# Quarter ends of an MLP: the next pair's first product moved between two parts of the last pair, and weight preparation moved behind the last minimum

## The chip, the cores and the metric

The kernel runs on one core of one Trainium2 chip. The metric is the time of one execution on the device, in microseconds (us); less is better. Engines are named as in the profile: PE is the matrix engine (matmuls; PEld its weight loads), DVE the vector engine, ACT the scalar engine, POOL and SP the two engines that mostly issue transfers here.

## The reference

One step of a two-layer encoder with model width 1024 and 576 tokens (512 of a prompt, 64 of a running stream). Layer 0 mixes tokens by causal pooling, layer 1 by sparse attention; each is followed by an MLP, and the change is in the MLP alone:

```python
def _mlp(h, w_up, w_down):          # w_up (1024, 4096), w_down (4096, 1024)
    u = jax.nn.relu(h @ w_up)
    return (u * u) @ w_down
...
x = x + _mlp(_rmsnorm(x, norm_mlp[i]), mlp_w_up[i], mlp_w_down[i])
```

## The kernel before

**Precision.** Every fp32 matmul is made of three: weights and operands are split into a high part (a cast) and a low part (value minus high part), and PE computes wh·uh, wh·ul and wl·uh. The cast is ACT's (for weights line 181, for activations `upper`, line 470), the subtraction DVE's (line 182 and `lower`, line 473). A weight *unit* is one 128x512 tile `wh` with its `wl`. There are six buffers for units (`UNITS = 6`), so the cast of a unit into `wh` waits until PE has read the unit six places earlier for the last time. `ahead()` makes the next unit if fewer than five (`LEAD`) stand ready, `take()` hands the oldest to a product.

**Seven products.** A 2x2 block product (halves of 576 tokens by pairs of weight blocks) is made by seven products instead of eight, named by the factor of the operand: b11, t1, t2, b21, t3, b22, t4. `seven()` issues them for one pair into three PSUM banks a, b and c: b11 into b (copied to a, line 530), t1 into c, t2 into b, then b21 into a, t3 into b, b22 into c, t4 into b. Each product is 4 k-parts (`rows`) of 3 matmuls of 128x288. A sink `on` takes the banks out when they are whole: `on.c`, `on.b`, `on.lo0`, `on.hi1`, `on.hi0`, `on.lo1`.

**Quarters.** The hidden width is worked in quarters c = 0 to 3. In c = 1 to 3 four `Up` pairs make activations (bank, times the norm, relu by a max or a min, square on ACT) and the operand `u` with its seven factors. `u` of pair j serves k-part j of the products of the `Down` pairs that follow, four of them (three for the last quarter of the last layer), which add to and subtract from the residual x (`update`, line 559). The end of a quarter is where the last `Up` pair (`final`) hands over to the first `Down` pair: that pair's products need `u` of the `Up` pair that is just being finished, so its k-part 3 comes late (`late`). There, t1 and t2 have their k-parts 0 to 2 first. There are six such ends: c = 1, 2, 3 in each of two layers. In the profiled execution they lie at 186, 277, 369, 834, 926 and 1017 us.

**Order.** Each engine works its own instructions in the order in which the program has them, and waits at one until its semaphores are there. The order is fixed when the program is built: a scheduler takes the operations by the order in which the code makes them and by what they depend on. The code's `with tc.issue_after(x)` puts what is made in it behind x on x's engine. Rows of the order below carry buffer numbers: at the end of the second quarter, `b_3498` (before) or `b_3504` (after) is the last `Up` pair's bank b, `b_3653`, `a_3654`, `c_3655` are the banks of the first `Down` pair, `u_3497` or `u_3503` is the operand that the last `Up` pair makes and `v_3496` or `v_3502` its values.

Of the kernel before, what the change touches and what calls it, by code (L numbers as in the profile page):

```python
# [12 lines left out]
ALU = mybir.AluOpType  # L13
# [43 lines left out]
def pool_dsa_kernel(ctx: ExitStack, tc: tile.TileContext, a, o):  # L57
# [53 lines left out]
    def f32(t):  # L111
        return t.bitcast(F32)
# [284 lines left out]
    def mlp(layer, gi, late=0, end=None):  # L397
# [74 lines left out]
        def lower(u, v, f):  # L472
            dve.tensor_tensor(u[:, f, 1], v[:, f], f32(u[:, f, 0]), ALU.subtract)  # L473

        def parts_of(u, v, f):

            upper(u, v, f)
            lower(u, v, f)

# [16 lines left out]
        def product(bank, w, operand, factor, js, first=False):  # L496
            for j in js:
                wh, wl = (t[:, j * P:(j + 1) * P] for t in w)
                uh, ul = (operand(j, factor, part) for part in range(2))
                for i, (wt, ut) in enumerate(((wh, uh), (wh, ul), (wl, uh))):  # L500
                    pe.matmul(bank[:, :HT], wt, ut, start=first and j == 0 and i == 0, stop=j == 3 and i == 2,  # L501
                              skip_group_check=True)

        tasks = [0]

        def ahead(n=1):

            how["sub"] = dve
            for _ in range(n):
                if len(ready) < LEAD:  # L510
                    u = next(units, None)
                    if u is not None:
                        ready.append(u)
# [6 lines left out]
        def seven(operand, late, on):  # L520
# [4 lines left out]
            w = take()  # L525
            product(b, w, operand, "b11", rows, True)
            tasks[0] += 1
# [5 lines left out]
            if late:  # L533
# [4 lines left out]
                on.c()  # L538
                ahead()
                product(b, w2, operand, "t2", rows[3:])  # L540
# [7 lines left out]
            for bank, factor, then in ((a_, "b21", on.lo0), (b, "t3", on.hi1), (c, "b22", on.hi0), (b, "t4", on.lo1)):  # L548
                product(bank, take(), operand, factor, rows)
                then()  # L550

        class Down:


            def __init__(self, q):
                self.lo, self.hi = ([x[2 * q + i][:, c0:c0 + HT] for i in range(2)] for c0 in (HT, 0))

            def update(self, to, bank, op):
                dve.tensor_tensor(to, to, self.banks[bank], op)  # L559

# [22 lines left out]
        class Up:  # L583
# [6 lines left out]
            def relu(self, i, src, op, h):  # L590
                v = self.v[:, i]
                dve.scalar_tensor_tensor(v, src, 0.0, halves(norm.rb)[:, h], op, ALU.mult)
                square(v)

            def c(self):
# [5 lines left out]
            def lo0(self):  # L601
                self.relu(4, self.banks[0], ALU.max, 1)
                ahead()
                if self.final:
                    parts_of(self.u, self.v, slice(4, 5))

            def hi1(self):
                v = self.v
                dve.tensor_tensor(v[:, 5], self.banks[1], snap[:, 0], ALU.add)  # L609
                self.relu(5, v[:, 5], ALU.min, 0)  # L610
                ahead()
# [11 lines left out]
            def lo1(self):  # L623
                v = self.v
                self.relu(6, self.banks[1], ALU.min, 1)
                if not self.final:
                    ahead()
                parts_of(self.u, v, slice(1, 4))
                last_sum(v)
                if not self.final:  # L630
                    ahead()
                parts_of(self.u, v, slice(0, 7, 6))
                if self.final:
                    ahead(2)

# [67 lines left out]
        for c in range(1, 4):  # L703
# [5 lines left out]
            if c < 3:  # L709
                for q in range(half):  # L710
                    seven(of(us), q == 0, Down(q))
        for q in range(pairs(3)):
            seven(of(us), q == 0, Down(q))
        if end:
# [865 lines left out]
```

## Time and profile before

| what | value |
|---|---|
| time, median of 3 runs | 1085.38 us (1085.03 to 1087.36) |
| profiled execution | 1086.18 us, with a span of 1084.4 us |
| PE busy | 1052.2 us, 97% of the span |
| DVE busy | 905.4 us, 83% |
| ACT busy | 627.7 us, 58% |
| mean granted clock of PE | 0.994 |

Times in rows are counted from the start of the span. The profiled execution took 1.8 us more than its span. PE is busy for all but 32 us, so only time in which PE waits, or in which its clock is lower, can be won; whether another engine is long busy matters only where PE waits for it. Matmuls overlap in the records: one takes 0.29 us, but the next starts 0.13 us after it.

### The profile page before, as it was taken

Reading aid. Unit: us, or ns where it says so; the run is one execution under the profiler, and the core shown is the slowest. Engines: PE = TensorE matmul, PEld = TensorE weight load, DVE = VectorE, ACT = ScalarE, POOL = GpSimd, SP = SyncE. Lnnn points to the kernel's source line nnn. Section 1 sums busy time; section 2 is a strip of 40 time slices with the busy share of each in tenths; the row PEclk is TensorE's granted clock in tenths of the full one; section 3 lists DMA queues with packets and bytes.
Section 4 is the critical chain, followed back from the end, with each engine's and each line's share of the span. In section 5 each row is a group of like instructions: output and inputs, shape, how many; then the busy total and the mean of one; then the engine's idle time right before and its main releaser. Section 6 shows DMA issues by size and latency. Waiting matters only on the chain.

```text
span 1084.4 us, 21653 instructions
## 1 busy us (share of the span) xinstructions
PE 1052.2 (97%) x7942; PEld 1024.4 (94%) x7942; DVE 905.4 (83%) x1837; ACT 627.7 (58%) x1240; POOL 263.9 (24%) x285
## 2 busy tenths in 40 slices
PE   9999999999999999999989999999999999999996
PEld 8999999999999999999979888999999999999895
DVE  7889889879978987869998944689889879979974
ACT  8556457447546654444477776456467447547641
POOL 3200111111111100227687892000111111111001
PEclk9999999999999999999999999999999999999998
DMA  8233776676676654456642454443775776676512
GB/s 252 91 100 89 173 163 160 162 164 165 154 165 166 156 161 165 126 155 186 200 113 66 136 161 127 126 108 89 175 162 150 172 167 164 152 170 157 128 50 88
DMA packets 94460, 157.66 MB, mean 145 GB/s; under 512 B 13730, under 2 KB 25297, under 8 KB 94353
## 3 DMA queue, kind: packets, MB, share of 16 engines
q1 hardware_dynamic: 68720, 109.80, 33.1%
q0 software_dynamic: 15840, 28.84, 17.4%
q10 hardware_dynamic: 9792, 17.63, 5.3%
q8 instruction: 62, 1.02, 0.4%
q14 instruction: 46, 0.37, 0.1%
HBM read 141.15 MB, written 10.89 MB: 140 GB/s over the span
## 4 chain that ended last, share of the span: by engine, by line
PE 78%; DVE 8%; DMA 4%; ACT 3%; issue 3%; POOL 2%; SPq 1%; DVEq 0%; POOLq 0%; ACTq 0%
PE b L501 29%; PE c L501 15%; PE up L305 9%; PE a L501 7%; PE pj L305 5%; PE wo L305 2%; PE wa L305 2%; DVE wl L182 2%; PE pb L1005 1%; PE pt L1304 1%; PE sc L1278 1%; PE o L1336 1%; PE dn L305 1%; DMA raw<-in_w_in 1%; DMA raw<-in_w_down 1%
## 5 line engine op out<-in xcount | busy, mean ns | idle before, releaser
L181 ACT CAST wh<-raw 128x512 fp32r<-128x512 f32 (+1 forms) x316 | 194.8, 620 | 250.8 <-PE b L501 84.4
L182 DVE TENSOR_TENSOR wl<-raw,wh 128x512 fp32r<-128x512 f32 (+1 forms) x294 | 206.1, 703 | 38.6 <-ACT wh L181 29.2
L501 PE MATMUL b<-u,wh 128*128 128x288 f32 x992 | 202.2, 296 | 3.6 <-ACT a L530 3.2
L501 PEld LDWEIGHTS b<-u,wh 128*128 128x128 f32 x992 | 159.0, 188 | 6.0 <-ACT a L530 6.0
L181 ACT CAST wh<-sum 128x512 fp32r<-128x512 f32 x165 | 101.7, 620 | 81.3 <-PE b L501 42.3
L501 PE MATMUL b<-u,wl 128*128 128x288 f32 x496 | 145.3, 295 | 0.0
L182 DVE TENSOR_TENSOR wl<-sum,wh 128x512 fp32r<-128x512 f32 x165 | 111.9, 687 | 26.3 <-ACT wh L181 24.0
L238 POOL DMA_DIRECT2D sum<-in_w_down x31 | 27.1, 891 | 329.0 <-DVE u L473 119.3
L501 PE MATMUL c<-u,wh 128*128 128x288 f32 x496 | 102.8, 296 | 0.1
L501 PEld LDWEIGHTS b<-u,wl 128*128 128x128 f32 x496 | 92.9, 188 | 0.0
L305 PE MATMUL up<-xs,wh 128*128 128x288 f32 x512 | 89.6, 296 | 0.9 <-DVE x L1471 0.8
L501 PE MATMUL b<-xt,wh 128*128 128x288 f32 x384 | 78.2, 297 | 6.7 <-DVE v L609 6.7
L473 DVE TENSOR_TENSOR u<-v,u 128x864 fp32r<-128x864 f32 (+2 forms) x100 | 81.7, 824 | 0.5 <-ACT u L470 0.5
L501 PEld LDWEIGHTS c<-u,wh 128*128 128x128 f32 x496 | 79.9, 188 | 1.3 <-DVE x L559 1.3
L501 PE MATMUL b<-xs,wh 128*128 128x288 f32 x384 | 77.2, 294 | 0.0
L305 PEld LDWEIGHTS up<-xs,wh 128*128 128x128 f32 x512 | 74.6, 188 | 2.0 <-ACT wh L181 1.0
L470 ACT CAST u<-v 128x864 fp32r<-128x864 f32 (+2 forms) x100 | 72.6, 729 | 4.3 <-DVE v L488 3.4
L501 PE MATMUL c<-u,wl 128*128 128x288 f32 x248 | 73.1, 295 | 0.0
L238 POOL DMA_DIRECT2D sum<-in_w_up x24 | 20.7, 863 | 211.5 <-DVE wl L182 120.5
L501 PEld LDWEIGHTS b<-xt,wh 128*128 128x128 f32 x384 | 61.5, 188 | 8.1 <-DVE v L609 8.1
L305 PE MATMUL pj<-xs,wh 128*128 128x288 f32 x352 | 61.3, 295 | 0.0
L501 PEld LDWEIGHTS b<-xs,wh 128*128 128x128 f32 x384 | 61.2, 188 | 0.0
(289 smaller groups left out, 2722.3 us busy)
## 6 DMA issues: line engine op xcount, KB each, us to landing
raw<-in_w_up SPq DMA_DIRECT2D x128, 256.0 KB, 3.0
raw<-in_w_down SPq DMA_DIRECT2D x128, 256.0 KB, 2.9
raw<-in_w_o ACTq DMA_DIRECT2D x32, 256.0 KB, 3.1
sum<-in_w_down SPq DMA_DIRECT2D x31, 256.0 KB, 2.8
sum<-in_w_down POOLq DMA_DIRECT2D x31, 256.0 KB, 4.8
raw<-in_w_down POOLq DMA_DIRECT2D x31, 256.0 KB, 5.1
raw<-in_w_in ACTq DMA_DIRECT2D x30, 256.0 KB, 3.4
sum<-in_w_up SPq DMA_DIRECT2D x24, 256.0 KB, 2.9
```

The lines of the kernel that those rows point to most:

```text
L181: act.copy(h, src)
L182: how["sub"].tensor_tensor(l, src, f32(h), ALU.subtract)
L238: pool.dma_start(s1, odd[:, 512:], accum_op=ALU.add)
L305: pe.matmul(pt[h][:, :m] if isinstance(pt, tuple) else pt[:, h, :m], wt, xs[k][:, part, c:c + m], start=(k == 0 and i == 0), stop=(k == n ...
L470: act.copy(u[:, f, 0], v[:, f])
L473: dve.tensor_tensor(u[:, f, 1], v[:, f], f32(u[:, f, 0]), ALU.subtract)
L501: pe.matmul(bank[:, :HT], wt, ut, start=first and j == 0 and i == 0, stop=j == 3 and i == 2, skip_group_check=True)
L1005: pe.matmul(pt[:, c0:c0 + rhs.shape[1]], lhs, rhs, start=n == 0, stop=n == len(steps) - 1)
L1278: pe.matmul(pt[:, hh, :nw], q[:, 2 * s + hh], ks[g][:, part, :nw], start=part == 0, stop=part == 1)
L1304: pe.transpose(pp[:, c:c + P], pr[:, hh, kt * P:(kt + 1) * P], ident)
L1336: pe.matmul(o[64 * hh:64 * hh + 64, s * P:(s + 1) * P], V[:, kt, vs], pT[:, c:c + P], start=kt == 0, stop=kt == i)
```

## The change

In `seven`, the first product b11 of the pair after a final `Up` is issued as a whole behind that `Up`'s product t3, so it lies between t3 and t4, which both go to the same bank b of the `Up` pair. For that, the parts of factor index 4 (b11) are made ahead of the sum of `hi1` (line 609 before, 624 after). From the last minimum of the final `Up` on (its relu of index 5, then the last parts in `lo1`), `ahead()` puts the DVE work of units behind a `gate`; the updates of x of the first `Down` pair stand behind the gate as well and become the gate themselves, so units that are made later stand behind them. The number of units made at the single places changes (`ahead(2)` after `on.c()`, one in `lo1`, none at its end). Lines from 501 on shift by 4 to 17.

```diff
         def ahead(n=1):
             how["sub"] = dve
             for _ in range(n):
                 if len(ready) < LEAD:
-                    u = next(units, None)
+                    with tc.issue_after(gate[0]) if gate else nullcontext():
+                        u = next(units, None)
...
             w = take()
-            product(b, w, operand, "b11", rows, True)
+            with tc.issue_after(behind.pop()) if late and behind else nullcontext():
+                product(b, w, operand, "b11", rows, True)
...
                 on.c()
-                ahead()
+                ahead(2)
                 product(b, w2, operand, "t2", rows[3:])
...
-                product(bank, take(), operand, factor, rows)
+                ins = product(bank, take(), operand, factor, rows)
+                if factor == "t3" and on.final:
+                    behind.append(ins.ins)
                 then()
...
             def update(self, to, bank, op):
-                dve.tensor_tensor(to, to, self.banks[bank], op)
+                with tc.issue_after(gate[0]) if self.late and gate else nullcontext():
+                    ins = dve.tensor_tensor(to, to, self.banks[bank], op)
+                if self.late and gate:
+                    gate[:] = [ins.ins]
...
                 if self.final:
-                    parts_of(self.u, self.v, slice(4, 5))
+                    self.first = parts_of(self.u, self.v, slice(4, 5))
...
-                dve.tensor_tensor(v[:, 5], self.banks[1], snap[:, 0], ALU.add)
-                self.relu(5, v[:, 5], ALU.min, 0)
+                with tc.issue_after(self.first.ins) if self.final else nullcontext():
+                    dve.tensor_tensor(v[:, 5], self.banks[1], snap[:, 0], ALU.add)
+                ins = self.relu(5, v[:, 5], ALU.min, 0)
+                if self.final:
+                    gate[:] = [ins.ins]
                 ahead()
...
                 self.relu(6, self.banks[1], ALU.min, 1)
-                if not self.final:
-                    ahead()
+                ahead()
                 parts_of(self.u, v, slice(1, 4))
...
-                parts_of(self.u, v, slice(0, 7, 6))
+                ins = parts_of(self.u, v, slice(0, 7, 6))
                 if self.final:
-                    ahead(2)
+                    gate[:] = [ins.ins]
...
-                    seven(of(us), q == 0, Down(q))
+                    seven(of(us), q == 0, Down(q, q == 0))
```

**PE, from the end of one product to t4, at the end of the second quarter.** Before (t3 is the run with `xs` and `wh_3514`, t4 begins with `xt_983`):

```order
L501 MATMUL b_3653<-u_3187,wh_3573 128x288 x2
L501 MATMUL b_3653<-u_3187,wl_3574 128x288
L501 MATMUL b_3653<-u_3342,wh_3573 128x288 x2
L501 MATMUL b_3653<-u_3342,wl_3574 128x288
L501 MATMUL b_3498<-xs_642,wh_3514 128x288 x2
L501 MATMUL b_3498<-xs_642,wl_3515 128x288
L501 MATMUL b_3498<-xs_645,wh_3514 128x288 x2
L501 MATMUL b_3498<-xs_645,wl_3515 128x288
L501 MATMUL b_3498<-xs_648,wh_3514 128x288 x2
L501 MATMUL b_3498<-xs_648,wl_3515 128x288
L501 MATMUL b_3498<-xs_651,wh_3514 128x288 x2
L501 MATMUL b_3498<-xs_651,wl_3515 128x288
```

Nine matmuls of b11 (bank `b_3653`) stand ahead of t3, and its last three, with `u_3497`, stand behind t4. The same place after, from the last part of t3 on:

```order
L501 MATMUL b_3504<-xs_651,wh_3494 128x288 x2
L501 MATMUL b_3504<-xs_651,wl_3495 128x288
L501 MATMUL b_3653<-u_3038,wh_3559 128x288 x2
L501 MATMUL b_3653<-u_3038,wl_3560 128x288
L501 MATMUL b_3653<-u_3193,wh_3559 128x288 x2
L501 MATMUL b_3653<-u_3193,wl_3560 128x288
L501 MATMUL b_3653<-u_3348,wh_3559 128x288 x2
L501 MATMUL b_3653<-u_3348,wl_3560 128x288
L501 MATMUL b_3653<-u_3503,wh_3559 128x288 x2
L501 MATMUL b_3653<-u_3503,wl_3560 128x288
L501 MATMUL b_3504<-xt_983,wh_3537 128x288 x2
```

All twelve matmuls of b11 have moved in between t3 and t4, those with the new operand `u_3503` among them.

**ACT, the casts of the last operand parts and of the next units, same end.** Before:

```order
L181 CAST wh_3705<-raw_3422 128x512
L530 COPY a_3654<-b_3653 128x288
L451 ACTIVATE v_3496<-v_3496 128x288
L470 CAST u_3497<-v_3496 128x3x288
L470 CAST u_3497<-v_3496 128x2x288
L181 CAST wh_3727<-raw_3489 128x512
L181 CAST wh_3746<-sum_3491 128x512
```

The two casts of operand parts, three factors and two factors wide, stand next to each other, and the unit for the next pair's b11 (`wh_3727`) comes behind them. After:

```order
L470 CAST u_3503<-v_3502 128x3x288
L181 CAST wh_3697<-sum_3557 128x512
L181 CAST wh_3701<-raw_3408 128x512
L451 ACTIVATE v_3502<-v_3502 128x288
L181 CAST wh_3714<-raw_3486 128x512
L470 CAST u_3503<-v_3502 128x2x288
L181 CAST wh_3733<-sum_3488 128x512
```

Three unit casts have moved in between the two casts of operand parts, the unit for the next pair's b11 (now `wh_3714`) among them.

**DVE, same end, from the last but one operand part to the third update of x.** Before:

```order
L473 TENSOR_TENSOR u_3497<-v_3496,u_3497 128x3x288
L473 TENSOR_TENSOR u_3497<-v_3496,u_3497 128x2x288
L559 TENSOR_TENSOR x_81<-x_81,c_3655 128x288
L559 TENSOR_TENSOR x_81<-x_81,b_3653 128x288
L182 TENSOR_TENSOR wl_3728<-raw_3489,wh_3727 128x512
L559 TENSOR_TENSOR x_81<-x_81,a_3654 128x288
```

After:

```order
L473 TENSOR_TENSOR u_3503<-v_3502,u_3503 128x3x288
L488 SCALAR_TENSOR_TENSOR v_3502<-v_3502 128x288
L473 TENSOR_TENSOR u_3503<-v_3502,u_3503 128x2x288
L182 TENSOR_TENSOR wl_3670<-raw_3386,wh_3669 128x512
L570 TENSOR_TENSOR x_81<-x_81,c_3655 128x288
L182 TENSOR_TENSOR wl_3698<-sum_3557,wh_3697 128x512
L182 TENSOR_TENSOR wl_3702<-raw_3408,wh_3701 128x512
L570 TENSOR_TENSOR x_81<-x_81,b_3653 128x288
```

The low part for t3 (`wl_3670`) has come in ahead of the update with bank c, and those for b22 and t4 (`wl_3698`, `wl_3702`) between it and the update with bank b. Before, all three stood further up: `wl_3670` right behind the sum of line 609, the other two ahead of the three-factor part. The rows ahead of that sum have lost four operations on units (lines 182 twice, 260 and 264), which now stand later.

Elsewhere, the scheduler's choice differs in places inside the attention layer (the order of some matmuls of the score, transpose and output products, of a few casts and of POOL's operations) and in the last products of the program; the work there is the same.

## Rows read from the trace of the kernel before

**Rows 1.** PE's waits over the whole execution: total us, times, longest

```profile
PE b L501 <- DVE v L609: 6.7, 6, 1.2
PE b L501 <- ACT a L530: 3.2, 7, 1.0
```

**Rows 2.** PE's timeline, end of the second quarter, first half: start us, length us

```profile
275.63 0.43 PE L501 MATMUL b<-xs,wh 128*128 128x288 f32 x2
...
277.09 0.29 PE L501 MATMUL b<-xs,wl 128*128 128x288 f32 x1
278.53 0.53 PE L501 MATMUL b<-xt,wh 128*128 128x288 f32 x2 [1.15 <-DVE v L609]
...
280.63 0.43 PE L501 MATMUL c<-u,wh 128*128 128x288 f32 x2
...
282.12 0.53 PE L501 MATMUL b<-u,wh 128*128 128x288 f32 x2
```

**Rows 3.** DVE's timeline, same end

```profile
276.69 0.69 DVE L264 TENSOR_TENSOR sum<-sum,raw 128x512 f32<-128x512 f32 x1
...
278.03 0.45 DVE L609 TENSOR_TENSOR v<-b,snap 128x288 f32<-128x288 f32 x1
...
283.51 1.72 DVE L473 TENSOR_TENSOR u<-v,u 128x864 fp32r<-128x864 f32 x2
285.48 0.46 DVE L559 TENSOR_TENSOR x<-x,c 128x288 f32<-128x288 f32 x1 [0.24 <-PE c L501]
285.85 0.45 DVE L559 TENSOR_TENSOR x<-x,b 128x288 f32<-128x288 f32 x1
286.21 0.69 DVE L182 TENSOR_TENSOR wl<-raw,wh 128x512 fp32r<-128x512 f32 x1
286.81 0.45 DVE L559 TENSOR_TENSOR x<-x,a 128x288 f32<-128x288 f32 x1
```

**Rows 4.** ACT's timeline, same end

```profile
277.29 0.62 ACT L181 CAST wh<-raw 128x512 fp32r<-128x512 f32 x1 [2.16 <-PE b L501]
277.84 0.44 ACT L451 ACTIVATE v<-v 128x288 f32<-128x288 f32 x1
...
283.63 0.67 ACT L470 CAST u<-v 128x576 fp32r<-128x576 f32 x1 [0.39 <-DVE v L488]
285.34 0.62 ACT L181 CAST wh<-raw 128x512 fp32r<-128x512 f32 x1 [1.04 <-PE c L501]
```

**Rows 5.** PE's timeline, same end, second half

```profile
284.61 0.29 PE L501 MATMUL c<-u,wh 128*128 128x288 f32 x1
...
285.01 0.29 PE L501 MATMUL c<-u,wh 128*128 128x288 f32 x1
...
285.99 0.53 PE L501 MATMUL c<-u,wh 128*128 128x288 f32 x2
286.36 0.29 PE L501 MATMUL c<-u,wl 128*128 128x288 f32 x1
...
287.69 0.69 PE L501 MATMUL b<-u,wh 128*128 128x288 f32 x4
```

**Rows 6.** PE's timeline, sixth end

```profile
1018.24 0.54 PE L501 MATMUL b<-xt,wh 128*128 128x288 f32 x2 [1.07 <-DVE v L609]
...
1022.67 0.53 PE L501 MATMUL b<-u,wh 128*128 128x288 f32 x2 [0.99 <-ACT a L530]
...
1029.29 0.42 PE L501 MATMUL b<-u,wh 128*128 128x288 f32 x2
```

**Rows 7.** Windows: length, busy PE, PEld, DVE, ACT, POOL, PE's clock, DMA share, GB/s

```profile
560.00:564.00 4.00, 2.19 (x16) 1.69 (x14) 3.86 (x11) 1.36 (x5) 2.55 (x3) 1.00 0.72 197
564.00:568.00 4.00, 2.31 (x12) 1.89 (x13) 3.96 (x14) 2.15 (x7) 1.98 (x2) 0.82 0.07 17
568.00:572.00 4.00, 4.00 (x21) 4.00 (x20) 2.74 (x13) 2.33 (x9) 3.84 (x4) 0.50 0.16 49
572.00:576.00 4.00, 4.00 (x29) 4.00 (x29) 2.94 (x11) 2.46 (x9) 0.89 (x1) 0.83 0.26 69
```

More of the change, by code (lines that the diff above doesn't have):

```diff
@@ L1 @@
-from contextlib import ExitStack, contextmanager
+from contextlib import ExitStack, contextmanager, nullcontext
 import numpy as np
@@ L472, in lower @@
         def lower(u, v, f):
-            dve.tensor_tensor(u[:, f, 1], v[:, f], f32(u[:, f, 0]), ALU.subtract)
+            return dve.tensor_tensor(u[:, f, 1], v[:, f], f32(u[:, f, 0]), ALU.subtract)
         def parts_of(u, v, f):
             upper(u, v, f)
-            lower(u, v, f)
+            return lower(u, v, f)
         def first_sum(v):
@@ L500, in product @@
                 for i, (wt, ut) in enumerate(((wh, uh), (wh, ul), (wl, uh))):
-                    pe.matmul(bank[:, :HT], wt, ut, start=first and j == 0 and i == 0, stop=j == 3 and i == 2,
-                              skip_group_check=True)
+                    ins = pe.matmul(bank[:, :HT], wt, ut, start=first and j == 0 and i == 0, stop=j == 3 and i == 2,
+                                    skip_group_check=True)
+            return ins
         tasks = [0]
+        gate = []
+        behind = []
         def ahead(n=1):
@@ L548, in seven, with __init__ @@
             for bank, factor, then in ((a_, "b21", on.lo0), (b, "t3", on.hi1), (c, "b22", on.hi0), (b, "t4", on.lo1)):
-                product(bank, take(), operand, factor, rows)
+                ins = product(bank, take(), operand, factor, rows)
+                if factor == "t3" and on.final:
+                    behind.append(ins.ins)
                 then()
         class Down:
-            def __init__(self, q):
+            final = False
+            def __init__(self, q, late=False):
+                self.late = late
                 self.lo, self.hi = ([x[2 * q + i][:, c0:c0 + HT] for i in range(2)] for c0 in (HT, 0))
             def update(self, to, bank, op):
-                dve.tensor_tensor(to, to, self.banks[bank], op)
+                with tc.issue_after(gate[0]) if self.late and gate else nullcontext():
+                    ins = dve.tensor_tensor(to, to, self.banks[bank], op)
+                if self.late and gate:
+                    gate[:] = [ins.ins]
             def c(self):
@@ L591, in relu @@
                 v = self.v[:, i]
-                dve.scalar_tensor_tensor(v, src, 0.0, halves(norm.rb)[:, h], op, ALU.mult)
+                ins = dve.scalar_tensor_tensor(v, src, 0.0, halves(norm.rb)[:, h], op, ALU.mult)
                 square(v)
+                return ins
             def c(self):
@@ L710, in mlp @@
                 for q in range(half):
-                    seven(of(us), q == 0, Down(q))
+                    seven(of(us), q == 0, Down(q, q == 0))
         for q in range(pairs(3)):
-            seven(of(us), q == 0, Down(q))
+            seven(of(us), q == 0, Down(q, q == 0))
         if end:
```

## The prediction

> **What bounds the kernel now.** PE is busy for 97% of the span, so the first view to read is the list of PE's waits. In it the reader should look at the two groups that belong to quarter ends [rows 1]: t4 waits for the sum of line 609, 6.7 us in six waits, 1.1 us each; and t2 waits for the copy of bank b into a, 3.2 us in seven waits. Other waits inside the MLP are small. The most that these places can give is therefore about 10 us, and what the change does is decided there, in PE's timeline of one end. I read the second end (276 to 288 us) because five of the six have the same rows, and the sixth, which carries extra work, by itself.
>
> In the first half of the end [rows 2] t3 is issued from 275.63 to 277.09, t4 comes only at 278.53, c's t1 at 280.63 and t2 at 282.12. Between the last matmul of t3 and t4 there are 1.44 us where a step is 0.13. DVE shows why [rows 3]: the sum of line 609 ran at 278.03 to 278.48, behind unit work that ended a step after 276.69, while t3 was long whole. In the second half [rows 5] the k-parts 3 begin at 284.61, b22 (which needs x to have taken bank c) at 285.99, and after it come two matmuls of the next b11 and then t3 (the row at 287.69 holds four, so t3 starts at 287.69 + 2 x 0.13 = 287.95). PE is nearly full there: b22 waits 0.18.
>
> **The change, front half.** I replay the end with the steps of these rows. t3 takes the place of the nine b11 matmuls ahead of it: start 275.63 - 9 x 0.1325 = 274.44. b11's first nine follow at 276.03 to 277.09, its first of part 3 at 277.22. What does part 3 wait for? In the order after, the cast of u for b11 stands on ACT behind a unit cast that waits for t3's last reading of its buffer. In the trace that cast began 277.29 - 275.63 = 1.66 after t3's start [rows 2, 4], so now at 276.10; the next ACT operation follows 0.55 later [rows 4], so the cast of u runs about 276.63 to 277.06, DVE's low part 277.10 to 277.55, and the sum of line 609 (now 624) a step of 0.37 behind it [rows 3], 277.47 to 277.92. PE goes on at 277.97 with t4 (releases in these rows take 0.04 to 0.05). That is 0.56 earlier than 278.53, with three b11 matmuls already done that stood behind t4, 0.40 more: c's t1 starts at 279.66 instead of 280.63. The copy into a is then ready, as b11 ended at 277.9 and t2 starts only at 280.85, so t2 has no wait and is 1.27 ahead; the k-parts 3 begin at 283.21, **1.40 ahead** of 284.61. So far the change does what it says. If the copy were late by what it was before, 0.31 of it would be lost.
>
> **The change, back half.** Here the reader should follow three rows of the order. On ACT, the unit cast for the next b11 (`wh_3714`) now stands ahead of the two-factor cast of u. It takes the buffer of the t1 unit, whose last reading is the second `c_3655` matmul of part 3. Before, the like cast waited 1.04 us for that matmul and nobody of this end was behind it: it began at 285.34, 0.33 after the matmul's issue at 285.01 [rows 4, 5]. Now that matmul is issued at 283.21 + 2 x 0.13 = 283.48 and the unit cast begins at 283.82; the two-factor cast starts a step of 0.53 later and takes 0.67 [rows 4], 284.35 to 285.02, where before it ran at 283.63. DVE's low part waits for it: 285.06 to 285.82. Then DVE does `wl_3670` (start 285.73, a step of 0.60 [rows 3]) ahead of the update of x with bank c: 286.33 to 286.79. b22 starts at **286.84, where it was 285.99**: the 1.40 that were won are gone, and 0.85 more.
>
> One term is still missing. b22's third matmul needs `wl_3698`, which stands behind that update on DVE: 286.70 to 287.39, so the third matmul comes at 287.44 instead of 286.36. After a wait, the first two matmuls here took 0.37 to the third instead of 0.27 [rows 5], so a second stop costs that 0.10 again: the fourth at 287.68, and t3 of this pair nine steps later at 288.87. Before it was 287.95. The update with bank b is done by 288.35 and holds nothing up. **One end loses 0.92 us.** What is behind it on DVE is about 1.6 us of unit work that has moved back; units stand up to five ahead, and I find no PE wait after that: `wl` of the next b11, read at about 290.4, is done by 289.5.
>
> Bounds of this term. If t4 waited for nothing at all, the front would gain another 0.35 and b22 would still be held by the chain cast, cast, low part, `wl`, update, which starts with a PE matmul: the loss is at least 0.45. If the sum of t4 came a step later on DVE (0.37) the loss grows to about 1.15 with the rounding of the steps. I take 0.92, since every duration in it has a row.
>
> **The sixth end** has four further casts and subtractions for the leftover columns. Before, t4 started at 1018.24, t2 waited 0.99 to 1022.67, t3 of the next pair started at 1029.29 [rows 6]. The same replay puts t4 at 1018.47 (ACT has two squares ahead of the cast of u here), so this front loses 0.23, then wins the copy's wait; the part 3 are at 1023.73, the unit cast at 1024.33. Here two unit casts, not one, stand ahead of the two-factor cast, which starts at 1025.38; b22 starts at 1027.87, its third matmul at 1028.47, the following t3 at 1029.90. Loss 0.61.
>
> **At nothing** I cost: the ends of quarter 0, whose `Down` pairs come without a final `Up` (PE's order there is the same up to the seed matmul, and its wait for the copy becomes one for x of the same length); the number of instructions, which is the same; and the transfers, which wait for the same buffers and have slack of several units. The changed order within attention touches 557 to 660 us, where PE is busy nearly throughout; I give it 0 with 1.5 us to either side.
>
> **Sum.** 5 x 0.92 + 0.61 = 5.2 us. The profiled execution took 1086.2, so it would take 1091.4; it lies 0.8 above the median of the runs, 1085.4, and against that the forecast is **1090.6 us**. With 6 x 0.45 and 6 x 1.15 for the ends, it spans 1088.1 to 1092.3. The measurement can tell about 0.2% of this kernel, 2.2 us, from no change.
>
> **Rivals.** *No change, 1085.0 (0.13).* It needs that the unit cast does not hold ACT up, as when the buffer it takes is free sooner than I read. Then the two-factor cast runs when its sum is there (283.39), the low part to 284.90, and b22 starts at 285.92, since `wl_3670` and the update on DVE still stand ahead of it: 0.07 better per end, 0.4 in all. For it speaks that DVE has work all the time in both versions; against it, the order of the buffers.
>
> *Faster, 1077 (0.05).* The 1.40 of the front stays whole in all six ends: 6 x 1.40 = 8.4. It decides if the update with bank c ends before 284.5, 1.4 before its time in rows 3; DVE would need to be 2.3 us ahead of my replay, and that I can't find in its rows.
>
> *The clock falls, 1094 or more (0.05).* Under attention, PE was busy for 4.5 of the 8 us from 560 on, and its clock then fell from full to half for about 1.4 + 4 + 1.4 = 6.8 us [rows 7]. That is 2.4 and then 1.2 GHz, and costs 3.4 us each time. In the changed ends PE would be busy for some 2.0 of 3.6 us, a like share, but over a stretch less than half as long. If the clock fell at one end, 1094; at all six, 1111.
> The Trainium skill (TensorE: Matmul & The Clock Gate, "Part 1: The HAM clock gate") says that the clock is halved after idling and released by activity; the rows at 560 agree, and by that rule alone every end with more waiting is a risk.
>
> *Attention, 1087 or 1094 (0.03).* The dip of rows 7 vanishes or doubles, 3.4 us either way.
>
> **Chances.** Forecast 0.74, no change 0.13, faster 0.05, clock 0.05, attention 0.03. The forecast and a clock that falls are slower by over 0.2%; so 0.79 slower, 0.15 same, 0.06 faster. The range reaches down to the case of no change and up past the bound of the sum: 1085.0 to 1092.6, which leaves out the faster case and the clock. The forecast's own range is 1088.1 to 1092.3.
>
> **What would show it.** In the changed trace: t4's wait gone or under 0.5 us, no wait for the copy at five ends; new PE waits at each end for `wh` of line 181 (about 0.5), for the two-factor low part (0.7), for x with bank c (0.6 to 0.9, where it was 0.18) and for `wl` (0.24); ACT's two-factor cast right behind a unit cast that waited for bank c. PE busy stays at 1052 us, and the ends are 0.9 us longer each. I am wrong if b22 begins at an end no later than before, counted from the end of the last `Up` pair's b22, or if ends grow shorter and time is lost elsewhere.

## The result, and the profile after

The changed kernel takes 1091.96 us (median of 4 runs, 1091.58 to 1092.81); the kernel before took 1086.37 us beside it (4 runs, 1085.03 to 1087.47). The ratio is 1.0052, with a 95% interval of 1.0040 to 1.0064: slower, 1.4 us above the forecast of 1090.6 and inside its range. Of these 1.4 us, 1.0 lies in the kernel before, which took 1086.37 us here and 1085.38 in the runs that the forecast started from. The profiled execution took 1091.58 us with a span of 1089.8, 5.4 us more than the span before.

The page's first part, after: busy time of each engine, share of the span, instructions.

```profile
PE 1058.1 (97%) x7942; PEld 1025.7 (94%) x7942; DVE 904.4 (83%) x1837; ACT 628.9 (58%) x1240; POOL 263.9 (24%) x285
```

The number of instructions on PE is the same, yet PE is busy for 5.9 us longer. Some matmuls ran longer, at a lower clock, as shown below; and a short stop counts as busy, since the record of a matmul lasts 0.29 us where the next can start after 0.13 us. The list of PE's waits after (total us, times, longest) answers to [rows 1]:

```profile
PE c L501 <- DVE x L570: 2.6, 6, 0.4
PE a L501 <- DVE u L473: 2.4, 6, 0.4
PE b L501 <- ACT wh L181: 1.9, 6, 0.3
...
PE b L501 <- ACT a L535: 0.9, 2, 0.5
```

t4's six waits for its sum are gone, and of the seven for the copy two are left, 0.9 us in all. Three groups of six have come in, one of each at every end: for x with bank c, for the last operand part, and for a unit's cast. Their totals don't say what they are worth, since they lie in one chain and the list counts a wait only from the modelled end of the last matmul. For that the second of the six ends has to be followed (c = 2, the one that the rows of the order call the end of the second quarter). PE's timeline there, which answers to [rows 2, 5]:

```profile
276.60 0.42 PE L501 MATMUL b<-xs,wh 128*128 128x288 f32 x2
...
279.36 0.78 PE L501 MATMUL b<-u,wh 128*128 128x288 f32 x2
...
280.12 0.53 PE L501 MATMUL b<-xt,wh 128*128 128x288 f32 x2
...
285.37 0.29 PE L501 MATMUL c<-u,wh 128*128 128x288 f32 x1
...
285.64 0.29 PE L501 MATMUL c<-u,wh 128*128 128x288 f32 x1
...
286.64 0.53 PE L501 MATMUL b<-u,wh 128*128 128x288 f32 x2 [0.31 <-ACT wh L181]
...
288.01 0.40 PE L501 MATMUL a<-u,wh 128*128 128x288 f32 x1 [0.40 <-DVE u L473]
...
288.98 0.53 PE L501 MATMUL c<-u,wh 128*128 128x288 f32 x2 [0.44 <-DVE x L570]
289.58 0.40 PE L501 MATMUL c<-u,wl 128*128 128x288 f32 x1
...
291.01 0.43 PE L501 MATMUL b<-u,wh 128*128 128x288 f32 x2
```

ACT's timeline, same end, which answers to [rows 4]:

```profile
284.63 0.44 ACT L451 ACTIVATE v<-v 128x288 f32<-128x288 f32 x1
285.97 0.62 ACT L181 CAST wh<-raw 128x512 fp32r<-128x512 f32 x1 [0.90 <-PE c L501]
286.49 0.67 ACT L470 CAST u<-v 128x576 fp32r<-128x576 f32 x1
```

DVE's timeline, same end, which answers to [rows 3]:

```profile
285.10 0.46 DVE L488 SCALAR_TENSOR_TENSOR v<-v 128x288 f32<-128x288 f32 x1
287.20 0.76 DVE L473 TENSOR_TENSOR u<-v,u 128x576 fp32r<-128x576 f32 x1 [1.63 <-ACT u L470]
287.87 0.69 DVE L182 TENSOR_TENSOR wl<-raw,wh 128x512 fp32r<-128x512 f32 x1
288.47 0.45 DVE L570 TENSOR_TENSOR x<-x,c 128x288 f32<-128x288 f32 x1
```

The three are read together, backwards from b22 at 288.98. It waits for the update with bank c (288.47), that stands behind a unit's low part (287.87) and the two-factor low part (287.20), this waits for the two-factor cast on ACT (286.49), and that stands behind a unit's cast which itself waited 0.90 us for a matmul of bank c, issued at 285.64. The values of the two-factor cast were there at 285.56 (285.10 + 0.46): ACT could have cast them 0.93 us earlier. Counted from start to start, less a step of 0.13 us, PE's stops are 0.47 us before 286.64, 0.66 before 288.01, 0.60 before 288.98 and 0.23 before 289.58; the forecast had about 0.5, 0.7, 0.6 to 0.9 and 0.24.

Counted from t3's first matmul, the forecast replay and the trace stand so (the replay's t3 at 274.44, the trace's at 276.60, later because the first end had lost time already):

| step | replay | trace |
|---|---|---|
| t4 | 3.53 | 3.52 |
| k-parts 3 | 8.77 | 8.77 |
| unit cast | 9.38 | 9.37 |
| two-factor cast | 9.91 | 9.89 |
| low part | 10.62 | 10.60 |
| update with bank c | 11.89 | 11.87 |
| b22 | 12.40 | 12.38 |
| its third matmul | 13.00 | 12.98 |
| next t3 | 14.43 | 14.41 |

At the sixth end the replay holds as well, until the clock falls there: from t3 (1014.22 in the replay, 1017.42 in the trace) to the first unit cast 10.11 and 10.13 us, to the two-factor cast 11.16 and 11.18, to b22 13.65 and 13.66, to its third matmul 14.25 and 14.26.

For the other ends I use the same measure for every kernel. All have 7942 matmuls on PE; the start of the n-th in one trace, less the start of the n-th in the trace before, is how far that trace is behind there. The growth of this between fixed places (the matmuls that before start at 172, 240, 330, 420, 700, 800, 890, 980 and 1050 us) is the loss of an end, or of attention (420 to 700). What is left to the difference of the spans, 0.2 us in the first row, lies outside of these stretches. "At half" is the time at half clock in the trace, worked out as below.

| profiled execution | end 1 | 2 | 3 | 4 | 5 | 6 | attention | at half | span |
|---|---|---|---|---|---|---|---|---|---|
| the change | 2.28 | 0.85 | 0.78 | 2.37 | 1.02 | 2.08 | -3.76 | 13.6 | 1089.8 |
| the change again | 2.56 | 0.89 | 0.99 | 1.03 | 1.03 | 2.07 | -2.23 | 13.6 | 1090.7 |
| before again | -0.06 | 0.02 | -0.05 | -0.01 | 0.04 | 0.01 | 0.07 | 6.8 | 1084.3 |
| one cast ahead | 0.09 | -0.01 | -0.13 | 0.12 | 0.10 | 0.19 | -1.31 | 3.4 | 1083.1 |
| update first | 0.99 | 0.88 | 0.95 | 1.08 | 1.02 | 0.59 | -2.74 | 0 | 1086.7 |
| all casts ahead | -0.48 | -0.55 | -0.62 | -0.49 | -0.37 | 0.10 | 0.79 | 13.6 | 1082.8 |
| layer 1 only | -0.02 | -0.01 | 0.05 | 1.18 | 1.03 | 2.03 | 0.63 | 13.6 | 1089.4 |
| all casts, b11 free | -0.03 | -0.04 | -0.17 | 0.02 | 0.15 | 1.25 | 0.11 | 13.6 | 1085.1 |
| b11 free | 2.45 | 0.82 | 0.74 | 0.98 | 0.98 | 1.95 | -2.56 | 13.6 | 1089.8 |
| casts and leftovers | -0.51 | -0.49 | -0.19 | -0.48 | -0.37 | -2.12 | -0.89 | 6.8 | 1079.1 |
| updates free | -0.56 | -0.65 | -0.65 | -0.49 | -0.49 | -1.06 | -0.37 | 6.8 | 1080.1 |
| units free of minimum | -0.14 | -0.07 | 0.03 | 0.05 | 0.25 | -0.43 | -2.79 | 6.8 | 1081.4 |

The first row has two surprises. Ends 1, 4 and 6 lost more than twice what the others did, and attention, which the change does not touch in the source, won 3.8 us. Windows of the changed kernel (columns as in [rows 7]) show both:

```profile
195.00:199.00 4.00, 3.65 (x15) 3.52 (x16) 4.00 (x8) 1.10 (x2) 0.00 (x0) 0.57 0.52 173
286.00:290.00 4.00, 2.75 (x13) 1.60 (x12) 2.80 (x5) 1.68 (x3) 0.00 (x0) 1.00 0.06 14
564.00:568.00 4.00, 1.60 (x11) 1.40 (x11) 3.90 (x12) 0.87 (x2) 2.50 (x2) 0.93 0.51 147
568.00:572.00 4.00, 4.00 (x27) 4.00 (x25) 3.96 (x19) 3.16 (x12) 2.94 (x3) 0.64 0.24 66
572.00:576.00 4.00, 4.00 (x32) 3.67 (x31) 4.00 (x14) 3.44 (x12) 3.84 (x3) 1.00 0.28 69
844.00:848.00 4.00, 4.00 (x19) 3.81 (x20) 3.50 (x7) 1.24 (x2) 0.00 (x0) 0.58 0.69 207
1032.00:1036.00 4.00, 4.00 (x21) 4.00 (x21) 2.76 (x6) 1.24 (x2) 0.66 (x1) 0.61 0.58 187
```

Right behind the first, fourth and sixth end the granted clock is 0.57, 0.58 and 0.61: part of each window at half clock (1.2 GHz instead of 2.4), (1 - 0.57) / 0.5 x 4 = 3.4 us in the first. Behind the second end (286 to 290) it stays at 1.00, and so it does behind the third and the fifth. Under attention the clock now is at half for (0.07 + 0.36) / 0.5 x 4 = 3.4 us, where [rows 7] give 6.8.

### The profile page after: what moved, and what is told of

Read it like the earlier page. It is cut to its first block, busy times and chain, and to the rows that moved or that the text cites. A ratio compares the mean times of both kernels' runs of the same rounds, so it can differ in the third digit from the quotient of the medians.

```text
span 1089.8 us, 21645 instructions
## 1 busy us (share of the span) xinstructions
PE 1058.1 (97%) x7942; PEld 1025.7 (94%) x7942; DVE 904.4 (83%) x1837; ACT 628.9 (58%) x1240; POOL 263.9 (24%) x285
## 3 DMA queue, kind: packets, MB, share of 16 engines
q8 instruction: 62, 1.02, 0.4%
## 4 chain that ended last, share of the span: by engine, by line
PE 79%; DVE 6%; issue 4%; DMA 4%; POOL 3%; ACT 2%; SPq 1%; POOLq 0%; DVEq 0%; ACTq 0%
PE b L501 31%; PE c L501 16%; PE up L305 9%; PE a L501 8%; PE wo L305 3%; PE pj L305 2%; PE wa L305 2%; PE sc L1294 1%; PE pb L1021 1%; PE pt L1320 1%; DVE wl L182 1%; PE dn L305 1%; PE o L1352 1%; POOL st L1122 1%; ACT wh L181 1%
## 5 line engine op out<-in xcount | busy, mean ns | idle before, releaser
L501 PE MATMUL b<-u,wh 128*128 128x288 f32 x992 | 205.8, 298 | 4.7 <-ACT wh L181 1.9
L501 PE MATMUL c<-u,wh 128*128 128x288 f32 x496 | 105.6, 303 | 2.6 <-DVE x L570 2.6
L501 PEld LDWEIGHTS c<-u,wh 128*128 128x128 f32 x496 | 82.4, 194 | 4.0 <-DVE x L570 4.0
L501 PE MATMUL c<-u,wl 128*128 128x288 f32 x248 | 75.8, 306 | 0.3
L570 DVE TENSOR_TENSOR x<-x,b 128x288 f32<-128x288 f32 x93 | 42.0, 451 | 23.9 <-PE b L501 23.5
```

What stands on the lines that cost most here:

```text
L501: ins = pe.matmul(bank[:, :HT], wt, ut, start=first and j == 0 and i == 0, stop=j == 3 and i == 2, skip_group_check=True)
L570: ins = dve.tensor_tensor(to, to, self.banks[bank], op)
```

## Experiments

The theory to be tested: the ends are longer because the two-factor cast of u stands on ACT behind a unit cast that waits for PE's last reading of a buffer; take that away and the loss goes. The rivals: the loss is DVE's (units ahead of the update of x), b11's new place itself, or it lies outside of the ends.

**One cast ahead.** The two-factor cast becomes a mark, behind which ACT puts the units from the fourth on that are made after it; DVE's order stays. `held()` is added to `ahead()`.

```diff
-                ins = parts_of(self.u, v, slice(0, 7, 6))
+                cast = upper(self.u, v, slice(0, 7, 6))
+                ins = lower(self.u, v, slice(0, 7, 6))
                 if self.final:
                     gate[:] = [ins.ins]
+                    casts[:] = [cast.ins, 0]
...
+        def held():
+            if casts and casts[1] < 3:
+                casts[1] += 1
+                return nullcontext()
+            return tc.issue_after(casts[0]) if casts else nullcontext()
```

> The changed kernel with one thing moved: at a quarter's end the unit cast for the next pair's b11, and the units made after it, stand behind ACT's two-factor cast of u instead of ahead of it; the three unit casts before it and DVE's order stay. Theory A (the end is set by the chain unit cast, two-factor cast, low part, update of x, b22, and the unit cast waits for a matmul of part 3): in the changed kernel's second end the two-factor cast began at 286.49, its sum was done at 285.56, so it can begin 0.9 sooner; the unit cast then comes some 0.2 later and PE's two matmuls that need it stop a little. Each end gets 0.6 to 0.9 shorter, together 4 to 5 us; the clock, which fell to half at the ends at 195, 844 and 1032 us, may stay up at some, 1.4 us each. Against the changed kernel's 1092.0: 1083 to 1088. Theory B (the loss comes from DVE, where unit work stands between the last low part and the updates of x): nothing changes on DVE, so 1092, at most 1 us less.

Measured: 1084.89 us beside 1086.60 before, ratio 0.9989 (0.9980 to 0.9998). Each end is back where it was before the change (-0.13 to 0.19), 0.86 to 0.92 us shorter than with it at ends 2, 3 and 5, and the clock falls at none. That the total is 1.7 us below the kernel before is not the ends' doing: in the trace attention won 1.31. DVE's order at the ends is that of the change; on PE the scheduler moved one matmul of bank a ahead of two of bank b there. ACT's timeline of this kernel at the second end:

```profile
283.30 0.67 ACT L470 CAST u<-v 128x576 fp32r<-128x576 f32 x1 [0.53 <-DVE v L488]
283.88 0.61 ACT L181 CAST wh<-raw 128x512 fp32r<-128x512 f32 x1
```

The two casts have changed places: the cast of u waits only for its values now. The loss is shown to be this order on ACT. But the 1.40 us that the front wins still don't arrive. PE's timeline of this kernel says what holds them:

```profile
283.38 0.29 PE L501 MATMUL c<-u,wh 128*128 128x288 f32 x1
...
285.79 0.53 PE L501 MATMUL c<-u,wh 128*128 128x288 f32 x2 [0.43 <-DVE x L577]
286.39 0.40 PE L501 MATMUL c<-u,wl 128*128 128x288 f32 x1
```

The k-parts 3 are early (this matmul was at 285.01 before), but b22 waits for the update, and its third matmul comes 0.60 behind its first instead of 0.37 [rows 5].

**Update first.** The change, but t3's unit is made behind `on.c()`, so that DVE has no unit ahead of the update with bank c.

```diff
-            ahead()
+            if not late:
+                ahead()
...
-                ahead(2)
+                ahead(3)
```

> The changed kernel with the unit for t3 made after bank c is taken, so that on DVE the update of x with bank c stands ahead of that unit's low part, and not behind it; ACT's order stays. Theory B: b22 starts a step of 0.60 sooner at each of six ends, 3.6 us together, 1088.4 or less. Theory A: b22 starts 0.6 sooner, but its third matmul needs the low part of its own unit, and that is not earlier (in the changed kernel it ended at 289.52 and the third matmul came at 289.58); PE stops there 0.6 to 0.7 longer. So 1092.0, within 1 us. If the clock falls at other ends than before, 1.4 us for each.

Measured: 1090.10 us beside 1086.60, ratio 1.0035 (1.0023 to 1.0047). The ends are as long as with the change (0.88 to 1.08 at five of them). The update and b22 did come earlier; DVE and PE of this kernel at the second end, and its list of PE's waits, show why it was worth nothing:

```profile
286.34 0.45 DVE L571 TENSOR_TENSOR x<-x,c 128x288 f32<-128x288 f32 x1
286.71 0.69 DVE L182 TENSOR_TENSOR wl<-raw,wh 128x512 fp32r<-128x512 f32 x1
287.31 0.68 DVE L182 TENSOR_TENSOR wl<-sum,wh 128x512 fp32r<-128x512 f32 x1
```

```profile
286.86 0.52 PE L501 MATMUL c<-u,wh 128*128 128x288 f32 x2
288.05 0.40 PE L501 MATMUL c<-u,wl 128*128 128x288 f32 x1 [0.68 <-DVE wl L182]
```

```profile
PE c L501 <- DVE wl L182: 4.0, 6, 0.7
```

b22's own low part of the weights is what comes late now: DVE has the same two operations behind the two-factor low part, in the other order, and b22 needs both by its third matmul. The total, 1090.1, lies between the two theories (1092 and 1088.4); by place it is theory A, with no fall of the clock in the trace. This trace is also the cleanest for the sum, though DVE's order differs from the change's: the clock stayed at full at all six ends and under attention, and the ends lose 5.5 us, where the forecast had 5.2.

**All casts ahead.** All instructions of the units made after the last operand parts stand behind the two-factor cast.

```diff
-                    with tc.issue_after(gate[0]) if gate else nullcontext():
+                    with tc.issue_after(gate[0]) if gate else nullcontext(), tc.issue_after(casts[0]) if casts else nullcontext():
...
+                    casts[:] = [cast.ins]
```

> The changed kernel with all units that are made after the last parts of the final Up held behind the two-factor cast of u on ACT, so the casts for t3, b22 and t4 as well. The scheduler then also puts the two updates of x ahead of these units on DVE. Theory A: the square ahead of the two-factor cast does not stand behind two unit casts any more (in the changed kernel's second end the square began at 284.63, its value was there at 284.07), the two-factor cast can begin when its sum is there and the update with bank c follows the low part at once. Each end gets about 1.5 us shorter, 9 us together; with so few stops the clock stays at full at all ends, another 4 us. 1077 to 1082, faster than both kernels. Theory B, in which ACT does not matter: only the 0.6 of the update at each end, 1088 to 1089.

Measured: 1081.94 us (12 runs, 1079.69 to 1087.57) beside 1086.60, ratio 0.9968 (0.9954 to 0.9981). The profiled execution, 1084.86, is not its median, so it is read by place: five ends are 0.4 to 0.6 us shorter than before, and ends 2, 3 and 5 are 1.4 shorter than with the change, close to the 1.5 expected. The clock did not stay at full as expected: it fell behind the sixth end and twice under attention, 13.6 us at half in all. ACT, DVE and PE of this kernel at the second end:

```profile
282.54 0.68 ACT L470 CAST u<-v 128x576 fp32r<-128x576 f32 x1 [0.89 <-DVE v L488]
283.12 0.61 ACT L181 CAST wh<-raw 128x512 fp32r<-128x512 f32 x1
```

```profile
283.25 0.76 DVE L473 TENSOR_TENSOR u<-v,u 128x576 fp32r<-128x576 f32 x1 [0.74 <-ACT u L470]
283.93 0.45 DVE L571 TENSOR_TENSOR x<-x,c 128x288 f32<-128x288 f32 x1
...
285.26 0.68 DVE L182 TENSOR_TENSOR wl<-raw,wh 128x512 fp32r<-128x512 f32 x1
```

```profile
284.52 0.50 PE L501 MATMUL c<-u,wh 128*128 128x288 f32 x2
284.86 1.02 PE L501 MATMUL b<-u,wh 128*128 128x288 f32 x4
285.99 0.40 PE L501 MATMUL b<-u,wl 128*128 128x288 f32 x1
```

With ACT's unit casts behind it, the cast of u waits for its values alone, the update follows the low part directly, and the matmul that waits for the update is issued at 284.52, where before it was at 285.99. Of these 1.47 us, 0.20 had been won when the end began (this trace started 0.28 late and won 0.48 at the first end), and 0.55 are this end's gain; the other 0.72 are lost again to new stops among the next matmuls, the last of which is the first with `wl`: it comes only at 285.99, when the low part made from 285.26 to 285.94 is there. That is where the rest of the front's gain stays.

**Layer 1 only.** The change in layer 1, the order of before in layer 0 (`new = layer == 1` on each of its conditions).

> The kernel before with the change in the second layer's MLP alone; ends 1 to 3 are as before. In the changed kernel the ends 1 to 6 lost 2.3, 0.9, 0.8, 2.4, 1.0 and 2.1 us (counted at the same matmuls of PE), and the attention between them won 3.8 us: its stretch at half clock was 3.4 us long, not 6.8, and some order differs. Theory A (the attention's gain comes from the order that the scheduler makes there when the first layer's end is changed): here attention is as before, 6.8 us at half clock, and the ends 4 to 6 lose 2.6 us without, 5.5 us with two falls of the clock: 1089 to 1092 beside 1086.4. Theory C (the attention's gain comes with the moment at which it starts, or by chance from run to run, and has nothing to do with the order): attention may win here as well, 1085 to 1088.

Measured: 1090.96 us beside 1086.60, ratio 1.0039 (1.0027 to 1.0052). Ends 1 to 3 are as before (-0.02 to 0.05), ends 4 to 6 as in the change, and attention, whose order is that of before here, wins nothing: it loses 0.63, with 10.2 us at half clock. So what attention won comes with the change of layer 0.

**All casts ahead, b11 free** and **b11 free.** In the first, b11 need not stand behind t3, with the ACT order mended as above; in the second, the same in the change itself.

```diff
-            with tc.issue_after(behind.pop()) if late and behind else nullcontext():
+            if behind:
+                behind.pop()
+            with nullcontext():
                 product(b, w, operand, "b11", rows, True)
```

> The kernel with all casts held behind the two-factor cast (1081.9 us), but b11 of the next pair not held behind t3: its first nine matmuls stand ahead of t3 again, as in the kernel before, and three between t3 and t4. Theory A (the front of the end is really won by b11's place, and the changed kernel loses it again behind ACT's unit cast): t3 is whole 9 x 0.13 = 1.2 us later, the sum of line 624 and DVE's chain behind it start later, part of it hidden by work that DVE has anyway; each end is 0.4 to 1.0 longer, the kernel 1084.5 to 1088. Theory D (b11's place is worth nothing, all of the gain of that kernel is the order on ACT and DVE): 1082, within 1 us.

> The changed kernel with b11 not held behind t3 and all else kept. Theory A: the end is set by ACT's unit cast and what hangs on it, and that waits for t1's part 3, which comes 0 to 0.3 later: 1091 to 1094, no better than the changed kernel. Theory E (the move of b11 is what costs: twelve matmuls, the last of which wait for the new operand, stand in front of t4): t4 starts sooner and each end gets 0.5 or more shorter, 1087 to 1089.

Measured: the first 1085.04 us beside 1085.88, ratio 0.9989 (0.9980 to 0.9998); the second 1090.95, ratio 1.0039 (1.0026 to 1.0053). With ACT mended, b11's place is worth 0.45 to 0.52 us at each of the first five ends (their row less that of "all casts ahead"), and 1.15 at the sixth, where the clock fell in both. In the change as it is, it is worth nothing: the ends are those of the change. The chain over ACT sets b22 whatever the front has won.

**Before again, the change again.** Both kernels unchanged, on the chip of the last two runs, which is another than that of the four runs ahead of them.

> The kernel before, unchanged, for a second profile of the same order. Theory C (the length of the stretch at half clock in attention differs from run to run): a stretch other than 6.83 us there, and attention's length moves with it. If it is the order alone: 6.83 us again, and the same places of all matmuls within 0.3 us.

> The changed kernel again, for a second profile of the same order and the spread of its times beside the kernel before on one chip. If the falls of the clock at ends come by chance (each end has the same stops, and in the first profile the clock fell at the ends at 195, 844 and 1032 us, 1.4 us each), they are at other ends or of another number now, and the ends without lose 0.8 to 1.0, the sixth 0.6. If they come from the order: the same three.

Measured: before 1086.13 us (one run); the change 1090.78 beside 1085.88, ratio 1.0039 (1.0026 to 1.0053). Before repeats to 0.1 us at each place. The change repeats at ends 2, 3 and 5, and not where the clock comes in; the windows of the second trace:

```profile
195.00:199.00 4.00, 3.49 (x16) 3.18 (x16) 4.00 (x9) 1.24 (x2) 0.00 (x0) 0.70 0.58 186
844.00:848.00 4.00, 3.06 (x17) 2.15 (x16) 3.75 (x7) 0.74 (x2) 0.00 (x0) 1.00 0.25 79
1032.00:1036.00 4.00, 3.93 (x17) 3.70 (x18) 3.67 (x7) 1.25 (x2) 0.00 (x0) 0.60 0.44 142
```

The clock fell again at ends 1 and 6 but stayed up at end 4, which then lost 1.03 instead of 2.37 us: the fall cost 1.3 there, by the same program.

**Casts and leftovers.** "All casts ahead" with `ahead(3)`, and the sixth end's leftover columns behind the gate and the cast too.

```diff
-                split(rest[j], parked[j // 2][:, j % 2, :HT])
+                with tc.issue_after(gate[0]), tc.issue_after(casts[0]):
+                    split(rest[j], parked[j // 2][:, j % 2, :HT])
```

> The kernel with all casts held behind the two-factor cast (1081.9), with two more things: three units instead of two made after bank c is taken, and at the last end the casts and subtractions of the leftover columns held behind the same cast and the updates of x. Theory A: the sixth end is held up by the leftovers in the same way (its two-factor cast and low part stand behind four of them), so it gets 1.0 to 1.5 shorter, and the clock may stay at full there, 1.4 more; the other ends win 0.1. Against the kernel with all casts held 1.5 to 3 less: 1079 to 1081. If leftovers are not what holds the sixth end: 1082.

Measured: 1080.88 us (5 runs, 1079.35 to 1081.26) beside 1086.24, ratio 0.9949 (0.9937 to 0.9961), the lowest median of all. The sixth end is 2.12 us shorter than before and 2.22 shorter than with "all casts ahead". Not all of this comes from the leftovers, since in that trace the clock fell behind the sixth end and here it did not; "updates free" below, which leaves the leftovers where they were and whose clock stayed up there, has -1.06, so that about half is theirs (an estimate, since DVE's order differs too). ACT there, in "all casts ahead" and then in this kernel:

```profile
1019.93 0.39 ACT L291 CAST xt<-rest 128x288 fp32r<-128x288 f32 x1
...
1022.28 0.67 ACT L470 CAST u<-v 128x576 fp32r<-128x576 f32 x1 [1.61 <-DVE v L488]
```

```profile
1019.14 0.67 ACT L470 CAST u<-v 128x576 fp32r<-128x576 f32 x1 [0.89 <-DVE v L488]
...
1021.80 0.39 ACT L291 CAST xt<-rest 128x288 fp32r<-128x288 f32 x1
```

**Updates free** and **units free of minimum.** Two parts of the change undone one at a time in "all casts ahead": the gate of the updates of x, and the gate at the last minimum (relu of index 5).

```diff
-                with tc.issue_after(gate[0]) if self.late and gate else nullcontext():
+                with nullcontext():
                     ins = dve.tensor_tensor(to, to, self.banks[bank], op)
-                if self.late and gate:
-                    gate[:] = [ins.ins]
```

```diff
-                ins = self.relu(5, v[:, 5], ALU.min, 0)
-                if self.final:
-                    gate[:] = [ins.ins]
+                self.relu(5, v[:, 5], ALU.min, 0)
```

> The kernel with all casts held (1081.9), without the part of the change that puts the updates of x behind the gate and units behind them. Theory A: once the casts are in order the scheduler puts the updates in front by itself or they have slack, so this part is worth nothing: within 1 us of 1082. If that part is worth what a step of DVE is at each end (0.6): 1085.5.

> The kernel with all casts held (1081.9), without the gate at the minimum of factor index 5: unit work on DVE may stand ahead of the sum of line 624 again, as in the kernel before. Theory A (the front is won by that): the sum waits for two or three unit operations of 0.6, part 3 of b11 comes 0.6 to 1.2 later, each end loses about 0.5 since DVE has the same work to do anyway: 1084 to 1086. If the gate is worth nothing: 1082.

Measured, beside 1086.24: 1081.89 us, ratio 0.9966 (0.9954 to 0.9978), and 1083.14, ratio 0.9978 (0.9966 to 0.9989). Without the gate of the updates nothing is lost: its first five ends are no longer than those of "all casts ahead". Without the gate at the minimum these ends are 0.34 to 0.65 us longer, as the theory had it (about 0.5). The total is below the theory's 1084 to 1086: in the one trace of each, attention came out 3.6 us shorter than with "all casts ahead", which hides part of the loss.

## Why the prediction was right

**Direction and mechanism** were right, and shown. The wait of t4 and most of the copy's went, the front came 1.40 us earlier, and all of it and 0.8 to 1.1 us more was lost behind one unit cast on ACT; every step of the replay came within 0.02 us. Moving that cast behind the operand's, and nothing on DVE, took the loss away.

**The term per end**, 0.92, measured 0.78 to 1.03 at the ends of the change whose clock stayed up, 0.88 to 1.08 in "update first", and 1.18 and 1.03 in "layer 1 only". The sixth, 0.61, measured 0.59 in "update first", the one version with the loss whose clock stayed up there; the sum of 5.2 us is 5.5 in that trace. The low part that I named ahead of the update (`wl_3670`) is worth nothing alone: putting the update first frees b22 by 0.6 but not its third matmul, which waits for `wl_3698`.

**The clock** was mis-sized, in chance and in price. I gave a fall 0.05, with the reason that the stretch with waiting is "less than half as long" as under attention. It fell at three ends of six in the one trace and at two in the other. That reason failed. The price of 3.4 us each was too high: behind an end the clock stays at half for 3.4 us and not 6.8, which on a full PE loses 1.7, and part of it lies in waits; 1.3 (end 4, by the same program) to 1.6 (end 1, 2.56 against the 0.99 of "update first") were measured. At the ends the two traces lost 9.38 and 8.57 us, 4.2 and 3.4 more than the forecast's 5.2. It is also part of why "PE busy stays at 1052 us" was wrong: 6.8 us more at half clock make up some 3.4 of the 5.9 us (an estimate for a full PE). The rest fits stops that count as busy: "update first", never at half, should by the clock alone be busy for less than the 1052.2 us of the kernel before, and has 1053.1.

**Attention** at 0 ± 1.5 was mis-sized too: it won 3.8 and 2.2 us. With layer 0 left as it was, it won nothing, so it comes with the scheduler's other order there: three traces with that order (the change twice, and "update first", whose order in attention is the same on every engine) won 2.2 to 3.8, and three with the order of before (twice the kernel before, and "layer 1 only") won nothing. The other versions have orders of their own there and lie between -2.8 and 0.8. Within one order the lengths do not follow the clock. The two traces of the change differ by 1.5 us, and at the matmul that before starts at 490 us they are already 1.33 apart (0.85 won, 0.48 lost), with the clock at full in both; the stretch at half clock comes only at 567 and 569 us. And "update first", never at half, won less than the trace with 3.4 us of it. Which of the moved rows wins was not tried and stays open.

So the total is near the forecast partly by luck, because two errors offset each other: +4.2 us for the clock and the ends' sizes (9.38 at the ends, less 5.2), -3.8 for attention in the profiled execution.

**The rivals.** "No change" asked that the unit cast not hold ACT; it held it for 0.9 us. "One cast ahead" is this rival made true, and it came out as priced: b22 starts 11.48 us after t3's first matmul (285.79 less 274.31), where the rival had 11.48 (285.92 less 274.44). "Faster" asked for an update with bank c before 284.5, or 10.06 after t3's first matmul: it ran from 11.87 to 12.32. Where ACT's and DVE's units both stood behind the cast ("all casts ahead", t3 at 274.22) it ran from 9.71 to 10.16, 0.10 short of that, and that version is faster, though by 0.5 us an end and not 1.4. Of "the clock falls" the event came and its price did not.

## What to carry to other kernels

An order that is set on one engine does not hold on the engine that feeds it: the gate put DVE's unit work behind the minimum, while ACT's half of the same units slipped ahead of the operand's cast, and one of them waited for a buffer. When an early start is bought for a bottleneck engine, follow the last operand through every helper engine and ask of each instruction ahead of it what that one waits for. Compare kernels at the same numbered matmul, place by place: totals here moved by 2 to 4 us for reasons that had nothing to do with the ends.

## What the runs showed of the hardware

The clock's fall is not the same thing each time. Of six ends with almost the same stops it fell at three and then at two; the ends that were spared twice (2, 3 and 5) have the same stops as end 1, which was hit in both traces (at end 1 the three waits of PE end at 193.02, 194.39 and 195.35, at end 2 at 286.64, 288.01 and 288.98: 1.37 and 0.96 or 0.97 apart). In "layer 1 only" it fell at end 6, and stayed up at end 4, which lost 1.18; in "b11 free" it fell at ends 1 and 6, and in "update first" at none. In the two traces of the change the stops behind which it fell are short: from start to start, less a step of 0.13 us, the longest is 0.66 us at ends 1 and 4 and 0.72 at end 6. At half clock a matmul follows the last after 0.24 us instead of 0.13, as these rows of the changed kernel behind its first end show on PE:

```profile
196.84 0.44 PE L501 MATMUL c<-u,wl 128*128 128x288 f32 x1
197.08 0.44 PE L501 MATMUL c<-u,wh 128*128 128x288 f32 x1
```

The Trainium skill (TensorE: Matmul & The Clock Gate, "Part 1: The HAM clock gate") says that idling halves the clock and activity releases it. The windows at 195, 844 and 1032 agree in that each follows an end with stops. What decides between equal stops, no run here shows. The same section of the Trainium skill says that the window in which the hardware looks at activity runs on freely and is not started anew by a kernel; by that it would matter where in a window an end falls, which fits an end that is hit in one execution and spared in the next, but was not tried.

The times of some versions spread more than those of others: "all casts ahead" ran from 1079.69 to 1087.57 us in 12 executions, "casts and leftovers" from 1079.35 to 1081.26 in five. The clock at the ends is not the whole of it: of the executions of "all casts ahead", the slowest has a mean granted clock of 0.986, but two with 0.993 took 1079.69 and 1085.14 us. What else differs between them is open; there is one trace of each version.
